# Hybrid decoder block: two of the attention's scans placed by hand in VectorE's order

## The chip, the cores and the metric

The kernel runs on one core of one Trainium2 chip, as one launch. The metric is the device time in microseconds (us). The engines are named as the profile names them: PE is TensorE, the matmul engine (PEld its weight loads), DVE is VectorE, ACT is ScalarE, POOL is GpSimd, SP is SyncE, which here issues the DMAs. All times on the trace are microseconds from the start of its span.

## What is computed

One layer of a hybrid decoder trunk over 1024 positions of width 1024: a token-mixing part (stick-breaking attention beside a Mamba-2 state-space mixer, SSD, gated and merged), cross-attention into 256 memory tokens, and a SwiGLU feed-forward, each between two RMS norms. The change touches the attention alone, 16 heads of 64 wide. For each head, query t and key s < t:

```python
z = q_t . k_s / sqrt(64)
beta = sigmoid(z)
A[t, s] = beta[t, s] * prod over s < j < t of (1 - beta[t, j])
o_t = sum over s < t of A[t, s] * v_s
```

so each row of the matrix of weights needs a running product from the diagonal leftwards over the keys.

## The kernel before

The sections follow one another: input norm and the first projections, convolution and gates (to about 655 us of the trace), the attention (657 to 1088 us, lines 750 to 954), the SSD section (from line 966), merge and output projection, cross-attention, feed-forward. Most matmuls are in fp32r and are done in three parts: an operand is split into a high part (rounded to fp32r) and a low part (what is left), and the products high x high, low x high and high x low are added up in PSUM.

**Attention.** The loop at L943 goes over 32 steps, m = 2h + half: head h, and the lower or upper 512 queries. Step m interleaves three lists of work in program order:

- `values(h, half)` (L880). For each block of 128 keys PE transposes the weights of up to four query blocks (L889) into a PSUM tile of a pool of two; ACT writes their high part `wth` (L892), DVE the low part `wtl` (L893, one input in PSUM and one in SBUF), and three blocks later PE multiplies both with the values, L901 for the high part and L902 for the low part. The lower half has four key blocks, the upper eight. Above the diagonal nothing is computed, so the last three low parts of each half have 384, 256 and 128 columns ("low384", "low256", "low128"), the others 512.
- `scores` of step m + 1 (L860). Query block b (0 to 7) has its scores against (b + 1) x 128 keys: matmuls L872 and L873, sigmoid on ACT (L874), and one scan on DVE (L875), in place on `n`, with the causal mask as second input: both inputs are in SBUF. The eight scans of a head have 128, 256, ... 1024 columns ("scan128" to "scan1024"). Those of 896 and 1024 columns belong to query blocks 6 and 7 and are issued in the step of the same head's lower half.
- one step of a dense projection (L772): q, k or gate columns of a later pair of heads. Its weight of 128 x 1024 is loaded by SP and split: the high part `whi` on ACT (L98) or on POOL (L94) in turn, the low part `wlo` on DVE (L101, two inputs in SBUF). What comes out is moved off PSUM by ACT, with a low part on DVE (L818 for q, L827 for k).

**Values.** `differences` (L845) makes the values' operand of a head on POOL: high part (L94) and low part (L101). Its tile comes from a pool of two, so it waits until PE's last product of the head before last. For every other head (a new pair) SP first loads `va` and `vb` (L851, one buffer each, free when the previous pair's low part is done), and POOL subtracts them (L852, 128 x 1024).

**Order.** What an engine executes, and in which order, is fixed when the kernel is built: a list scheduler with its own estimates of durations starts what it takes to be ready first and prefers earlier program text. So an instruction may be placed far ahead of its place in the text: the scans of 896 and 1024 columns of a head stand ahead of the last low parts of the previous head. `behind(marks)` (L204) is a context in which instructions are issued after the marked ones. When both are on one engine it sets only their order and needs no semaphore. "Head change" below means the stretch in which PE ends the values of head h - 1 and begins those of head h.

Of the kernel before, what the change touches and what calls it, by code (L numbers as in the profile page):

```python
# [8 lines left out]
F32 = mybir.dt.float32  # L9
# [3 lines left out]
ALU = mybir.AluOpType  # L13
# [3 lines left out]
P = 128  # L17
S = 1024
# [16 lines left out]
def hybrid_block(ctx, tc, a, out, dbg=None):  # L35
    nc = tc.nc
    V, A, G, T = nc.vector, nc.scalar, nc.gpsimd, nc.tensor
# [11 lines left out]
    def mk(pl, shape, dt, tag, bufs=None):  # L49
        uid[0] += 1  # L50
        kw = {} if bufs is None else {"bufs": bufs}
        return pl.tile(shape, dt, tag=tag, name=f"{tag}_{uid[0]}", **kw)
# [151 lines left out]
    def behind(marks):  # L204

        st = ExitStack()
        for m in marks:
            st.enter_context(tc.issue_after(m.ins))
        return st
# [45 lines left out]
    with ExitStack() as pa:  # L255
# [24 lines left out]
        with ExitStack() as p1:  # L280
# [135 lines left out]
            pt = mk(psp, [P, HALF], F32, "pdt", bufs=1)  # L416
# [4 lines left out]
            pt = mk(psp, [P, HALF], F32, "pv")  # L421
# [328 lines left out]
        with ExitStack() as p2:  # L750
# [13 lines left out]
            mask = mk(cb_, [P, S], BF16, "mask")  # L764
            V.memset(mask, 0.0)
            G.affine_select(mask[:, S - P:], mask[:, S - P:], [[-1, P]], ALU.is_gt, 1.0, base=0, channel_multiplier=1)

            marks, sig = [], []
            PIN = 8
            FQ = 1  # L770

# [73 lines left out]
            def differences(h):  # L845

                j = h % 2
                if j == 0:
                    va, vb = [mk(vp, [P, NCH, P], F32, n, bufs=1) for n in ("va", "vb")]
                    for t, r in ((va, 0), (vb, 1)):  # L850
                        nc.sync.dma_start(t, v_d[r:S + r, h * HD:(h + 2) * HD].rearrange("(c p) d -> p c d", p=P))  # L851
                    G.tensor_tensor(va, va, vb, ALU.subtract)  # L852
                    dvs[0] = va
                dv = dvs[0][:, :, j * HD:(j + 1) * HD]
                vt = mk(vp, [P, NCH, P], F32R, "v")
                hi_sb(vt[:, :, 0:HD], dv, "p")
                lo_of(vt[:, :, HD:P], dv, vt[:, :, 0:HD], G)
                heads[h]["v"] = vt

            def scores(h, half, tb, ns_):  # L860
                def run():
                    hd = heads[h]
                    if half == 0 and tb == 0:
                        differences(h)
                    b = half * 4 + tb
                    L = (b + 1) * P
                    nt = mk(bp, [P, (half + 1) * HALF], F32, f"n{half}")
                    ns_.append(nt)
                    for s0 in range(0, L, HALF):
                        s1 = min(L, s0 + HALF)  # L870
                        ps = mk(psc, [P, HALF], F32, "sc")[:, :s1 - s0]
                        T.matmul(ps, hd["qs"][:, b * P:(b + 1) * P], hd["kh"][:, s0:s1], start=True, stop=False)  # L872
                        marks.append(T.matmul(ps, hd["qs"][:, b * P:(b + 1) * P], hd["kl"][:, s0:s1], start=False, stop=True))  # L873
                        sig.append(A.activation(nt[:, s0:s1], ps, AF.Sigmoid, scale=-(HD ** -0.5)))  # L874
                    V.tensor_tensor_scan(nt[:, 0:L][:, ::-1], nt[:, 0:L][:, ::-1], mask[:, S - L:][:, ::-1], 1.0, ALU.mult, ALU.max)  # L875
                return run

            LAG = 3
# [1 line left out]
            def values(h, half, ns_):  # L880

                st = {}
                ni = 4 * (half + 1)

                def tr(i):
                    t0 = max(0, i - 4 * half)
                    pt = mk(pst, [P, HALF], F32, "tr")
                    for tb in range(t0, 4):
                        T.transpose(pt[:, tb * P:(tb + 1) * P], ns_[tb][:, i * P:(i + 1) * P], ident)  # L889
                    wh = mk(wt, [P, HALF], F32R, "wth")  # L890
                    wl = mk(wt, [P, HALF], F32R, "wtl")
                    A.activation(wh[:, t0 * P:], pt[:, t0 * P:], AF.Identity, bias=mone)  # L892
                    V.scalar_tensor_tensor(wl[:, t0 * P:], pt[:, t0 * P:], -1.0, wh[:, t0 * P:].bitcast(F32), ALU.add, ALU.subtract)  # L893
                    st[i] = (wh, wl, t0 * P)

                def av(i):
                    if i == 0:
                        st["po"] = mk(psv, [P, HALF], F32, "av")
                    po, vt = st["po"], heads[h]["v"]
                    wh, wl, off = st[i]  # L900
                    T.matmul(po[:, off:], vt[:, i, :], wh[:, off:], start=i == 0, stop=False)  # L901
                    marks.append(T.matmul(po[:, off:], vt[:, i, :], wl[:, off:], start=False, stop=i == ni - 1))  # L902
                    if i == ni - 1:
                        o = mk(t2, [P, HALF], F32, "oT")
                        A.activation(o, po, AF.Copy)
                        for j in range(2):
                            nc.sync.dma_start(o_d[j][h * HD:(h + 1) * HD, half * HALF:(half + 1) * HALF], o[j * HD:(j + 1) * HD])

                def step(i):
                    def run():  # L910
                        if i < ni:
                            tr(i)
                        if i >= LAG:
                            av(i - LAG)
                    return run

                return [step(i) for i in range(ni + LAG)]

            def interleave(*lists):
                items = []  # L920
                for n, (l, a0, a1) in enumerate(lists):
                    for i, f in enumerate(l):
                        items.append((a0 + (a1 - a0) * (i + 0.5) / len(l), n, f))
                for _, _, f in sorted(items, key=lambda t: t[:2]):
                    f()

            def qk_quanta(hp):

                if hp >= NH // 2:
                    return [[]] * 4  # L930
                q, k = qk_proj(hp)
                n = KT // FQ + 1
                return [q[:n], q[n:] + k[:1], k[1:n], k[n:]]
# [9 lines left out]
            for m in range(NM):  # L943
                h, half = m // 2, m % 2
                hp, r = m // 4, m % 4
                s1 = [scores((m + 1) // 2, (m + 1) % 2, tb, ns_[m + 1]) for tb in range(4)] if m + 1 < NM else []
                if r == 3:
                    nxt = qk_quanta(hp + 2)
                dn = nxt[(r + 1) % 4]
                if m >= NM - 5:  # L950
                    n = -(-len(late) // (NM - m))
                    dn, late = late[:n], late[n:]
                interleave((values(h, half, ns_[m]), 0, 1), (s1, 0, 0.7), (dn, 0, 1))
# [13 lines left out]
    with ExitStack() as p3:  # L967
# [36 lines left out]
        marks = []  # L1004
# [391 lines left out]
    marks = []  # L1396
# [506 lines left out]
```

## Time and profile before

| | us |
|---|---|
| median of 3 runs | 2554.7 |
| lowest and highest | 2552.59, 2555.76 |
| the profiled execution, device time | 2557.21 |
| its span in the trace | 2555.4 |

The profiled execution is one more run, recorded by the hardware profiler. Its span runs from the first to the last recorded instruction; durations below come from it. A row of a timeline gives start, duration, engine, line, operation, what comes out and goes in (partitions x elements), how many instructions the row joins, and in brackets how long the engine had been idle and what ended that. A row of the list of waits gives engine and tile that waited, what for, microseconds in total, times, and the longest or the mean of one. Engines work at the same time, so busy shares do not add up, and idle time of an engine that is not the bottleneck costs nothing.

### The profile page before, as it was taken

To read this page: it belongs to the slowest core of one execution; us is meant where nothing else is said; L and a number is where in the kernel's file an instruction comes from. 1 tells how busy PE (TensorE), PEld (TensorE's weight loads), DVE (VectorE), ACT (ScalarE), POOL (GpSimd) and SP (SyncE) were. 2 spreads that over 40 slices of the span, in tenths; PEclk is the share of its full clock that TensorE was granted. 3 is DMA by queue.
4 is the path that set the end of the run, shared out by engine and by line. 5 is a ranking of instruction groups with operands and counts; after the bars stand their busy time and mean duration, and the time that the engine had idled before them with its cause. 6 is when DMAs were issued, how large, how long until landed. Compare 5 with 4: busy or idle time off the path is not lost. (4 is left out here: it accounts for less than half of the span.)

```text
span 2555.4 us, 33383 instructions
## 1 busy us (share of the span) xinstructions
PE 2475.9 (97%) x12378; PEld 2033.6 (80%) x12378; DVE 1772.8 (69%) x2093; ACT 1133.7 (44%) x2023; POOL 853.9 (33%) x650
## 2 busy tenths in 40 slices
PE   7999999999999999999999999999999999999998
PEld 5788888887888878777777788887787888888876
DVE  7665777767578787688888664316459666666997
ACT  5333455555456665566554213215233333334343
POOL 3221544443121211256656040101113333323772
PEclk9999999999999999999999999999999999999999
DMA  7431443332543434365332662311232232224232
GB/s 246 152 116 55 138 149 99 99 112 90 153 112 87 120 99 104 100 207 168 107 106 65 203 209 83 124 50 34 99 116 66 83 91 75 90 91 165 99 132 99
DMA packets 255275, 293.51 MB, mean 115 GB/s; under 512 B 17023, under 2 KB 175240, under 8 KB 254986
## 3 DMA queue, kind: packets, MB, share of 16 engines
q1 hardware_dynamic: 255114, 291.40, 36.6%
q8 instruction: 97, 1.59, 0.3%
q14 instruction: 64, 0.52, 0.1%
HBM read 200.10 MB, written 74.45 MB: 107 GB/s over the span
## 5 line engine op out<-in xcount | busy, mean ns | idle before, releaser
L875 DVE TENSOR_TENSOR_SCAN n<-n,mask 128x128 f32<-128x128 f32 (+7 forms) x128 | 181.7, 1445 | 23.4 <-ACT n L874 22.2
L101 DVE TENSOR_TENSOR sw<-sf,sw 128x512 fp32r<-128x512 f32 x150 | 120.9, 818 | 82.0 <-ACT sw L98 80.5
L892 ACT ACTIVATE wth<-tr,mone 128x512 fp32r<-128x512 f32 x192 | 110.2, 584 | 81.4 <-PE tr L889 80.6
L98 ACT ACTIVATE sw<-sf 128x512 fp32r<-128x512 f32 x150 | 92.1, 626 | 113.0 <-PE mm L217 97.8
L183 POOL TENSOR_TENSOR sf<-wr,wr 128x512 f32<-128x512 f32 x38 | 59.4, 1563 | 233.4 <-DMA wr<-in_w_gu_dram 116.7
L893 DVE SCALAR_TENSOR_TENSOR wtl<-tr,wth 128x512 fp32r<-128x512 f32 x192 | 99.3, 544 | 53.9 <-ACT wth L892 53.8
L98 ACT ACTIVATE sw<-wr 128x512 fp32r<-128x512 f32 x113 | 71.2, 631 | 126.2 <-PE mm L217 125.6
L217 PE MATMUL mm<-h,sw 128*128 128x512 f32 x320 | 125.0, 392 | 1.8 <-DVE sw L101 1.8
L215 PE MATMUL mm<-h,sw 128*128 128x512 f32 x320 | 122.6, 391 | 2.9 <-ACT h L98 2.3
L216 PE MATMUL mm<-h,sw 128*128 128x512 f32 x320 | 125.3, 391 | 0.0
L101 DVE TENSOR_TENSOR sw<-wr,sw 128x512 fp32r<-128x512 f32 x113 | 106.6, 945 | 21.1 <-ACT sw L98 21.0
L669 DVE SCALAR_TENSOR_TENSOR b<-b,prmT,b 128x1023 f32<-128x1023 f32 (+2 forms) x72 | 109.6, 1522 | 15.1 <-ACT b L667 14.5
L94 POOL TENSOR_SCALAR v<-va 128x512 fp32r<-128x512 f32 x16 | 20.6, 1289 | 278.2 <-PE av L902 164.0
L874 ACT ACTIVATE n<-sc 128x512 f32<-128x512 f32 (+1 forms) x192 | 88.6, 494 | 45.5 <-PE tr L889 28.8
L152 POOL TENSOR_SCALAR rstd<-ms 128x1 f32<-128x1 f32 x74 | 28.1, 379 | 237.1 <-ACT x L1414 110.3
L104 PE MATMUL mm<-oth,bw 128*128 128x512 f32 x256 | 103.6, 405 | 3.6 <-DVE a L1214 3.6
L104 PE MATMUL p<-bw,h 128*128 128x512 f32 x256 | 98.7, 391 | 3.3 <-DVE x L1416 2.4
L105 PE MATMUL mm<-otl,bw 128*128 128x512 f32 x256 | 100.5, 393 | 0.0
L106 PE MATMUL mm<-oth,bw 128*128 128x512 f32 x256 | 100.4, 392 | 0.0
L106 PE MATMUL p<-bw,h 128*128 128x512 f32 x256 | 100.1, 392 | 0.0
L105 PE MATMUL p<-bw,h 128*128 128x512 f32 x256 | 99.9, 390 | 0.0
L185 POOL TENSOR_TENSOR sf<-wr 128x512 f32<-128x512 f32 x38 | 63.0, 1657 | 105.4 <-DVE sw L101 105.4
(616 smaller groups left out, 8044.0 us busy)
## 6 DMA issues: line engine op xcount, KB each, us to landing
wr<-in_w_gu_dram SPq DMA_DIRECT2D x80, 256.0 KB
wr<-in_w_in_dram SPq DMA_DIRECT2D x36, 512.0 KB
zr<-in_w_in_dram SPq DMA_DIRECT2D x28, 512.0 KB
gu_d<-t SPq DMA_DIRECT2D x44, 256.0 KB
wraw<-in_w_in_dram SPq DMA_DIRECT2D x20, 512.0 KB
zs_d<-zo SPq DMA_DIRECT2D x32, 256.0 KB
xs_d<-b SPq DMA_DIRECT2D x32, 256.0 KB
kl<-gt SPq DMA_DIRECT2D x64, 128.0 KB
```

The costliest lines, as they stand in the source:

```text
L98: A.activation(o, i, AF.Copy)
L101: eng.tensor_tensor(o, i, hi.bitcast(F32), ALU.subtract)
L104: first = T.matmul(ps, sh, mh, start=start, stop=False)
L105: T.matmul(ps, sh, ml, start=False, stop=False)
L106: T.matmul(ps, sl, mh, start=False, stop=stop)
L215: T.matmul(ps, w[0][:, k, :], bh, start=first and k == 0, stop=False, skip_group_check=True)
L216: T.matmul(ps, w[0][:, k, :], bl, start=False, stop=False, skip_group_check=True)
L217: ins = T.matmul(ps, w[1][:, k, :], bh, start=False, stop=last and k == 3, skip_group_check=True)
L669: V.scalar_tensor_tensor(acc[:, sh:], y[:, :S - sh], cw(3 - sh, f), acc[:, sh:], ALU.mult, ALU.add)
L875: V.tensor_tensor_scan(nt[:, 0:L][:, ::-1], nt[:, 0:L][:, ::-1], mask[:, S - L:][:, ::-1], 1.0, ALU.mult, ALU.max)
L892: A.activation(wh[:, t0 * P:], pt[:, t0 * P:], AF.Identity, bias=mone)
L893: V.scalar_tensor_tensor(wl[:, t0 * P:], pt[:, t0 * P:], -1.0, wh[:, t0 * P:].bitcast(F32), ALU.add, ALU.subtract)
```

## The change

The list `lows` collects every low-part instruction of L893. At the start of each step of the loop, `lows_done` notes the last one of the steps before and how many there are by then. In `scores`, the scan of query block 6 (896 columns) is issued behind that last low part, which in the step of a head's lower half is low128 of the previous head's upper half. The scan of query block 7 (1024 columns) is issued behind the first low part that is added after the note, the first low part (512 columns) of this head's lower half. For the first head both lists are empty. No instruction is added or taken away, and the scheduler places everything else anew around the two ties. After line 875 the changed file's lines stand one further down, after line 946 two.

```diff
-            marks, sig = [], []
+            marks, sig, lows, lows_done = [], [], [], []
...
-                    V.tensor_tensor_scan(nt[:, 0:L][:, ::-1], nt[:, 0:L][:, ::-1], mask[:, S - L:][:, ::-1], 1.0, ALU.mult, ALU.max)
+                    with behind(lows_done[:1] if b == 6 else lows[lows_done[1]:][:1] if b == 7 and lows_done else []):
+                        V.tensor_tensor_scan(nt[:, 0:L][:, ::-1], nt[:, 0:L][:, ::-1], mask[:, S - L:][:, ::-1], 1.0, ALU.mult, ALU.max)
...
-                    V.scalar_tensor_tensor(wl[:, t0 * P:], pt[:, t0 * P:], -1.0, wh[:, t0 * P:].bitcast(F32), ALU.add, ALU.subtract)
+                    lows.append(V.scalar_tensor_tensor(wl[:, t0 * P:], pt[:, t0 * P:], -1.0, wh[:, t0 * P:].bitcast(F32), ALU.add, ALU.subtract))
...
             for m in range(NM):
                 h, half = m // 2, m % 2
                 hp, r = m // 4, m % 4
+                lows_done[:] = [lows[-1], len(lows)] if lows else []
```

## The prediction

> **What bounds the kernel now.** The page comes first. TensorE (PE) is busy 97% of the span, no other engine comes near, so an edit counts only by what it does to PE's waits. The change issues the same instructions in another order, so nothing is gained in work. The second view is the list of waits over the attention section (657 to 1055 us), because it says which of PE's waits end on VectorE (DVE).
>
> ```profile
> span 2555.4 us, 33383 instructions
> PE 2475.9 (97%) x12378; PEld 2033.6 (80%) x12378; DVE 1772.8 (69%) x2093; ACT 1133.7 (44%) x2023; POOL 853.9 (33%) x650
> PE av L902 <- DVE wtl L893: 7.3, 6, 1.2
> PE tr L889 <- DVE wtl L893: 0.8, 2, 0.5
> ```
>
> Six times PE stands 1.2 us before the L902 matmul for a low part of L893, and twice 0.4 us on average in its transposes: 8.1 us is all that a better DVE order can win from PE here. The timelines show where. There are fifteen head changes, some 25 us apart, and they alternate. In six of them (702, 752, ... 952 us; call them A) POOL also splits a weight. In six more (725, 775, ... 975; call them B) ACT splits the weight, and POOL goes on to the next pair's subtraction L852. The remaining three are irregular. Here is A, on DVE, POOL, ACT and PE:
>
> ```profile
> 747.97 3.66 DVE L875 TENSOR_TENSOR_SCAN n<-n,mask 128x768 f32<-128x768 f32 x2
> 752.07 2.28 DVE L875 TENSOR_TENSOR_SCAN n<-n,mask 128x1024 f32<-128x1024 f32 x1
> 755.54 1.16 DVE L875 TENSOR_TENSOR_SCAN n<-n,mask 128x256 f32<-128x256 f32 x1
> 757.97 1.23 DVE L101 TENSOR_TENSOR wlo<-wraw,whi 128x1024 fp32r<-128x1024 f32 x1 [0.82 <-POOL whi L94]
> 759.71 0.95 DVE L875 TENSOR_TENSOR_SCAN n<-n,mask 128x384 f32<-128x384 f32 x1
> 760.58 0.59 DVE L893 SCALAR_TENSOR_TENSOR wtl<-tr,wth 128x256 fp32r<-128x256 f32 x2
> ...
> 754.05 0.71 POOL L94 TENSOR_SCALAR v<-va 128x512 fp32r<-128x512 f32 x1 [14.13 <-PE tr L889]
> 754.85 1.30 POOL L101 TENSOR_TENSOR v<-va,v 128x512 fp32r<-128x512 f32 x1
> 756.88 1.05 POOL L94 TENSOR_SCALAR whi<-wraw 128x1024 fp32r<-128x1024 f32 x1 [0.73 <-PE mm L105]
> ...
> 749.85 0.37 ACT L892 ACTIVATE wth<-tr,mone 128x128 fp32r<-128x128 f32 x1 [0.44 <-PE tr L889]
> ...
> 752.00 0.38 PE L902 MATMUL av<-wtl,v 128*128 128x256 f32 x1 [1.23 <-DVE wtl L893]
> 761.47 0.28 PE L902 MATMUL av<-wtl,v 128*128 128x256 f32 x1
> ```
>
> The first row is two scans, 768 then 896 columns, ending at 751.63; only then come the low parts, and PE waits to 752.00. And B:
>
> ```profile
> 723.75 3.68 DVE L875 TENSOR_TENSOR_SCAN n<-n,mask 128x768 f32<-128x768 f32 x2
> 727.34 0.60 DVE L893 SCALAR_TENSOR_TENSOR wtl<-tr,wth 128x256 fp32r<-128x256 f32 x2
> 728.22 2.98 DVE L875 TENSOR_TENSOR_SCAN n<-n,mask 128x1024 f32<-128x1024 f32 x2 [0.28 <-ACT n L874]
> 731.12 1.12 DVE L893 SCALAR_TENSOR_TENSOR wtl<-tr,wth 128x512 fp32r<-128x512 f32 x2
> 732.82 1.22 DVE L101 TENSOR_TENSOR wlo<-wraw,whi 128x1024 fp32r<-128x1024 f32 x1 [0.58 <-ACT whi L98]
> 733.97 0.68 DVE L818 TENSOR_TENSOR gt<-mm,qs 128x512 fp32r<-128x512 f32 x1
> 734.57 1.53 DVE L875 TENSOR_TENSOR_SCAN n<-n,mask 128x256 f32<-128x256 f32 x2
> 736.01 0.60 DVE L893 SCALAR_TENSOR_TENSOR wtl<-tr,wth 128x256 fp32r<-128x256 f32 x2
> 736.52 1.22 DVE L875 TENSOR_TENSOR_SCAN n<-n,mask 128x512 f32<-128x512 f32 x1
> 786.51 3.12 DVE L875 TENSOR_TENSOR_SCAN n<-n,mask 128x512 f32<-128x512 f32 x1
> ...
> 728.89 2.05 POOL L94 TENSOR_SCALAR v<-va 128x512 fp32r<-128x512 f32 x1 [20.65 <-PE av L902]
> 731.02 1.30 POOL L101 TENSOR_TENSOR v<-va,v 128x512 fp32r<-128x512 f32 x1
> 736.60 3.32 POOL L852 TENSOR_TENSOR va<-va,vb 128x1024 f32<-128x1024 f32 x1 [4.28 <-DMA va<-v_d]
> 786.16 2.39 POOL L852 TENSOR_TENSOR va<-va,vb 128x1024 f32<-128x1024 f32 x1 [3.83 <-DMA va<-v_d]
> ...
> 726.85 0.37 ACT L892 ACTIVATE wth<-tr,mone 128x128 fp32r<-128x128 f32 x1 [1.11 <-PE tr L889]
> ...
> 732.34 0.37 SPq L851 DMA_DIRECT2D va<-v_d  x1
> ...
> 737.27 0.28 PE L902 MATMUL av<-wtl,v 128*128 128x256 f32 x1
> ```
>
> **Scans and POOL shut each other out.** These rows decide the sign. POOL's high part takes 0.71 us in A; in B it starts 0.67 us into scan1024 (728.22, alone 2.28, so ending 730.50), takes 2.05 and ends at 730.94, 0.44 after the scan. The scan of 128 behind it ends at 731.20, 0.70 after scan1024. Scan256 of A starts while POOL's L101 runs (754.85 to 756.15) and ends at 756.70, 0.55 after it; a free pair of 256 and 384 takes 1.53, so with 0.95 less some 0.1 of overlap for 384 it is 0.68 for 256 alone. At 786.16 the subtraction came first (ends 788.55) and scan512 took 3.12 instead of 1.22, ending 1.08 later; at 736.60 the scan came first (ends 737.74) and the subtraction took 3.32 instead of 2.39, ending 2.18 later. So whoever starts first keeps the other off, and a blocked scan ends after POOL by its own time less 0.14. The Trainium skill, page "SBUF — State Buffer", section "Who interferes with whom", says that a DVE instruction with two SBUF inputs contends with a GpSimd instruction that reads SBUF, and that whoever issues first keeps the shared ports while the other fully blocks. The trace agrees on who wins; the tail of a blocked POOL part is 0.44 where the rule's whole 0.71 would stand, and with whole durations each B below would cost some 0.5 us more.
>
> **The change part by part.** It ties scan896 of head h behind the last low part of head h-1, and scan1024 behind the first low part of head h. DVE's new order at a head change is scan768, low256, low128, scan896, scan128, low512, scan1024, low384, then the weight's low part, L818 or L827, scan256, scan384, low256. What is queued behind the tied scans is therefore all of that, and PE waits for it at the second low256.
>
> *A.* Low128 follows its high part (750.22) and ends at 750.52; scan896, 2.0 us, runs 750.45 to 752.45, and PE's L902 goes at 750.6, 1.4 early. POOL's high part, freed by PE's last product, comes earlier with it, now falls into scan896 and ends at 752.45 + 0.44 = 752.9; scan128 ends at 753.15, low512 (0.6) at 753.7. POOL's L101 runs 752.95 to 754.25, as it does before 0.1 behind the high part. Scan1024 is queued at 753.7, in the middle of it, and ends at 754.25 + 2.14 = 756.4; before, it ran free. POOL's weight part, ready about 755.5 (1.4 earlier than its row), is shut out by it and ends at 757.35 (1.05 less some 0.1). Low384 fits in that gap; the weight's low part 757.35 to 758.6, L827 (0.6 net) 759.2, scan256 759.8, scan384 760.65, the first low256 to 760.95. PE takes it at 761.0 where it took it at 761.47. So of 1.4 us 0.95 is given back: **-0.45 each, six times -2.7**. Bounds: -7.3 if nothing blocks (the wait row whole); 0 if POOL's high part loses to scan128, which starts within 0.2 us of it, since the chain is then 0.4 later.
>
> *B.* The low parts wait for their high part anyway (727.22), so PE wins 0.3. Low128 ends at 727.55, scan896 runs 727.5 to 729.5, POOL's high part, freed at 728.6, ends 729.95, scan128 730.2, low512 730.75. POOL's L101 runs 730.0 to 731.3; scan1024, queued at 730.75, ends at 731.3 + 2.14 = 733.45. Low384 to 733.9, the weight's low part (before 732.82, waiting for ACT) 733.85 to 735.05, L818 735.65, scan256 queued at 735.6, 1.0 later than before. The DMA L851 is issued at the end of L101 (732.34 against 732.32), so it goes 1.0 earlier, and the subtraction is ready 3.83 to 4.28 after that end: 735.15 to 735.6 instead of 736.60. It used to fall behind scan384 (ends 736.10); now it meets scan256. If it is first, it ends at about 737.8, scan256 at 738.35, scan384 (0.85) 739.2. If scan256 is first, the subtraction ends 2.18 after it, at 738.45, and scan384 at 739.15. Either way the first low256 is there at 739.6, and PE wanted it at 737.27: **+2.3 each, six times +13.8**, from 0 (it lands after scan384 as before) to 2.8 (the subtraction at 735.6 and as long as in its longest row here, 3.32, so until 738.9, 0.5 later). The 0.8 us of the transposes' wait goes, since it came of the subtraction ahead of scan512: **-0.8**.
>
> *The last head,* at 1065 us, where DVE has slack and scan1024 fills it:
>
> ```profile
> 1065.29 2.89 DVE L875 TENSOR_TENSOR_SCAN n<-n,mask 128x1024 f32<-128x1024 f32 x1 [2.66 <-ACT n L874]
> 1070.90 2.35 DVE L1047 TENSOR_TENSOR colrows<-ident 16x1024 fp32r<-16x1024 f32 x2
> 1073.28 0.43 DVE L893 SCALAR_TENSOR_TENSOR wtl<-tr,wth 128x256 fp32r<-128x256 f32 x1
> 1073.71 1.28 DVE L1017 SCALAR_TENSOR_TENSOR wraw<-wraw,rstd,wraw 128x1024 f32<-128x1024 f32 x1
> ...
> 1075.53 0.28 PE L902 MATMUL av<-wtl,v 128*128 128x128 f32 x1
> ```
>
> Tied, scan1024 waits for a low512 that is ready only about when the scan now ends, so all of its 2.3 us comes on top: low256 ends near 1075.8 instead of 1073.71, and the order puts both L1017 (1.28 each) ahead of low128, which then ends near 1078.6. PE wanted that at 1075.53: +3.1, less some 0.5 for a wait there that the later second L1017 caused. I take **+2.5**, from 1.6 (low256 alone) to 3.1. At the irregular change near 1005 POOL's high part is long already, 1.45 us:
>
> ```profile
> 1005.11 1.45 POOL L94 TENSOR_SCALAR v<-va 128x512 fp32r<-128x512 f32 x1 [15.23 <-PE av L902]
> ```
>
> I take the middle between none and one B there, **+1.1**, and 0 at the one near 1028, where PE waits for no low part.
>
> *What else the order moves.* The 256-column scores of A go behind nine projection matmuls, one gate store on SP goes ahead of two loads, all with microseconds of slack: 0. In the SSD section a few transposes and two small products go behind other matmuls, sign unknown: 0. The stretch there has this room, so I allow 4 us to either side:
>
> ```profile
> 1090.00:1180.00 90.00, 81.31 (x627) 66.63 (x626) 78.56 (x84) 56.45 (x98) 51.57 (x41) 0.98 0.66 201
> ```
>
> The columns are the stretch, its length, busy time of PE, PE's weight loads, DVE, ACT and POOL. PE idles 8.7 us of 90.
>
> **The sum.** 13.8 - 0.8 - 2.7 + 2.5 + 1.1 = +13.9 us. The profiled run took 2557.2 for a span of 2555.4; the median of the three runs shown is 2554.7. Adding the difference to that gives 2568.6, say **2568 us**.
>
> **The rivals.**
> *The waits go and nothing follows.* The subtraction lands outside the scans and A's POOL parts do not block: -7.3 - 0.8 + 2.5 = -5.6, 2549 us. For it speaks that the subtraction misses the scans today by only 0.5 us, so small shifts decide; against it, that the two shifts (DVE 1.0 later, POOL 1.0 earlier) both push it in, and either order of arrival gives the same end. Chance 0.13.
> *Gain and loss cancel.* B is free, A gains its 2.7, the last head and 1005 cost 3.6, the transposes' 0.8 goes: 0, 2555 us. This needs the subtraction later than 736.1 on the new clock, a load 0.5 us longer than the slowest row. Chance 0.14.
> *Worse still.* As forecast, but POOL's high part loses to scan128 in A (gain 0) and the SSD section loses 4: 2568.6 + 2.7 + 4 = 2575 us. For it, the race within 0.2 us; against, no row of the SSD stretch. Chance 0.13.
> That the order does not change is ruled out: the instruction lists show it at all fifteen head changes.
>
> **How the numbers follow.** The forecast keeps 0.60. What a measurement of this kernel can tell from no change is about 0.2%, 5.1 us. Slower is forecast and worse, 0.73; same 0.14; faster 0.13. The forecast's own range is 2561 to 2573; the range of 8 in 10 takes in the worse case and reaches down towards the cancelled one: 2553 to 2577.
>
> **What would show it.** A: no wait on L902 at 752, scan1024 of some 2.7 us queued behind L101, and the second low256 within 0.5 us of its old place against PE. B: a new PE wait of about 2 us at L902 for L893, six times, near 737 plus the drift, with scan256 or scan384 stretched to over 2 us beside L852. The last head: a PE wait near 1078. If L852 starts behind scan384, B's 13.8 falls and I am wrong on the side of the rivals; if scan1024 runs free, A's gain is larger than I say.

## The result and the profile after

The changed kernel takes 2573.0 us (median of 6 runs, 2572.1 to 2578.6) against 2556.0 for the kernel before in 6 runs: a ratio of 1.0068, 95% interval 1.0057 to 1.0079, so it is slower by 17 us. The forecast was 2568 with a range of 2553 to 2577; the result lies 5 us above the forecast, at the upper end of its narrower range (2561 to 2573).

The head of its page, and from its list of waits (657 to 1110 us) the two that end on low parts (these are now L894, their products L903, the transposes L890, the scans L876):

```profile
span 2571.8 us, 33367 instructions
PE 2477.2 (96%) x12378; PEld 2033.4 (79%) x12378; DVE 1784.4 (69%) x2093; ACT 1132.1 (44%) x2023; POOL 857.6 (33%) x650
...
PE av L903 <- DVE wtl L894: 20.7, 14, 2.4
PE tr L890 <- DVE wtl L894: 0.5, 2, 0.3
```

The same 12378 matmuls are as busy as before. Over the same 657 to 1110 us the kernel before has 7.3 and 1.8 us in these two rows, so PE's waits for low parts have grown from 9.1 to 21.2 us. That the loss lies in the attention is seen from the rows of the low products, grouped by line, before and after. The times in them are the starts of the first and the last:

```profile
L902 PE MATMUL av<-wtl,v x192: 221/422/667, 682.2 to 1087.8; 128*128 128x512 f32 x96, 128*128 128x384 f32 x32, 128*128 128x256 f32 x32, 128*128 128x128 f32 x32
```

```profile
L903 PE MATMUL av<-wtl,v x192: 222/422/668, 679.7 to 1102.2; 128*128 128x512 f32 x96, 128*128 128x384 f32 x32, 128*128 128x256 f32 x32, 128*128 128x128 f32 x32
```

From the first to the last it is 405.6 us before and 422.5 after, +16.9. This stretch is used below for every run, since it leaves out what lies ahead of the attention: the first low product comes at 675.6 to 680.8 us in the ten runs below, whatever was changed in them, and at 682.2 in the trace of before. Each stretch comes from one execution, so it also holds what PE's clock did in it (last section).

**B, after** (DVE, POOL, PE at 725 us; columns as before):

```profile
724.80 2.70 DVE L876 TENSOR_TENSOR_SCAN n<-n,mask 128x896 f32<-128x896 f32 x2
728.01 2.76 DVE L876 TENSOR_TENSOR_SCAN n<-n,mask 128x1024 f32<-128x1024 f32 x1
732.87 3.53 DVE L876 TENSOR_TENSOR_SCAN n<-n,mask 128x256 f32<-128x256 f32 x2
736.32 0.59 DVE L894 SCALAR_TENSOR_TENSOR wtl<-tr,wth 128x256 fp32r<-128x256 f32 x2
...
727.32 1.30 POOL L101 TENSOR_TENSOR v<-va,v 128x512 fp32r<-128x512 f32 x1
732.62 2.38 POOL L852 TENSOR_TENSOR va<-va,vb 128x1024 f32<-128x1024 f32 x1 [4.00 <-DMA va<-v_d]
...
736.77 0.39 PE L903 MATMUL av<-wtl,v 128*128 128x256 f32 x1 [2.22 <-DVE wtl L894]
```

The subtraction starts at 732.62, a quarter of a microsecond before scan256; the pair of 256 and 384, 1.53 before, takes 3.53, and PE stands 2.22 us. Scan1024 is shut out behind L101 on the way (2.76 for 2.28).

**A, after** (750 us):

```profile
750.07 2.33 DVE L876 TENSOR_TENSOR_SCAN n<-n,mask 128x896 f32<-128x896 f32 x2
752.90 2.28 DVE L876 TENSOR_TENSOR_SCAN n<-n,mask 128x1024 f32<-128x1024 f32 x1
757.32 1.23 DVE L101 TENSOR_TENSOR wlo<-wraw,whi 128x1024 fp32r<-128x1024 f32 x1 [1.70 <-POOL whi L94]
760.51 0.60 DVE L894 SCALAR_TENSOR_TENSOR wtl<-tr,wth 128x256 fp32r<-128x256 f32 x2
...
751.98 0.83 POOL L94 TENSOR_SCALAR v<-va 128x512 fp32r<-128x512 f32 x1 [16.98 <-PE av L903]
752.90 3.37 POOL L101 TENSOR_TENSOR v<-va,v 128x512 fp32r<-128x512 f32 x1
756.24 1.05 POOL L94 TENSOR_SCALAR whi<-wraw 128x1024 fp32r<-128x1024 f32 x1
...
760.97 0.38 PE L903 MATMUL av<-wtl,v 128*128 128x256 f32 x1 [0.80 <-DVE wtl L894]
```

Scan1024 and POOL's L101 both start at 752.90. The scan has its free 2.28, and L101 takes 3.37 instead of 1.30; the weight's high part stands behind it, DVE waits 1.70 us for that, and PE 0.80 at the second low256. From the second low256 product of B to that of A it is 761.47 - 737.27 = 24.20 before and 760.97 - 736.77 = 24.20 after: A wins nothing and loses nothing. POOL's L101 takes 3.36 to 3.38 us in all six A.

### The profile page after: what moved, and what is told of

Same layout as the page of the kernel before. It is cut to its first block, busy times and chain, and to the rows that moved or that the text cites. A ratio compares the mean times of both kernels' runs of the same rounds, so it can differ in the third digit from the quotient of the medians.

```text
span 2571.8 us, 33367 instructions
## 1 busy us (share of the span) xinstructions
PE 2477.2 (96%) x12378; PEld 2033.4 (79%) x12378; DVE 1784.4 (69%) x2093; ACT 1132.1 (44%) x2023; POOL 857.6 (33%) x650
## 3 DMA queue, kind: packets, MB, share of 16 engines
q8 instruction: 97, 1.59, 0.3%
## 5 line engine op out<-in xcount | busy, mean ns | idle before, releaser
L876 DVE TENSOR_TENSOR_SCAN n<-n,mask 128x128 f32<-128x128 f32 (+7 forms) x128 | 187.4, 1486 | 11.9 <-ACT n L874 8.6
L101 DVE TENSOR_TENSOR sw<-sf,sw 128x512 fp32r<-128x512 f32 x150 | 121.8, 824 | 80.7 <-ACT sw L98 79.2
L893 ACT ACTIVATE wth<-tr,mone 128x512 fp32r<-128x512 f32 x192 | 110.3, 585 | 105.5 <-PE tr L890 104.9
L894 DVE SCALAR_TENSOR_TENSOR wtl<-tr,wth 128x512 fp32r<-128x512 f32 x192 | 101.6, 546 | 75.1 <-ACT wth L893 74.9
L101 DVE TENSOR_TENSOR sw<-wr,sw 128x512 fp32r<-128x512 f32 x113 | 107.3, 951 | 21.4 <-ACT sw L98 21.3
L94 POOL TENSOR_SCALAR v<-va 128x512 fp32r<-128x512 f32 x16 | 15.1, 948 | 290.5 <-PE av L903 290.4
L903 PE MATMUL av<-wtl,v 128*128 128x512 f32 x192 | 78.0, 407 | 20.9 <-DVE wtl L894 20.7
```

Source lines behind the costliest of these rows:

```text
L101: eng.tensor_tensor(o, i, hi.bitcast(F32), ALU.subtract)
L894: lows.append(V.scalar_tensor_tensor(wl[:, t0 * P:], pt[:, t0 * P:], -1.0, wh[:, t0 * P:].bitcast(F32), ALU.add, ALU.subtract))
```

## The experiments

Each run is compared with runs of the kernel before on its own chip; "stretch" is the one above, 405.6 before and 422.5 for the changed kernel.

**1. A short subtraction.**

```diff
-                    G.tensor_tensor(va, va, vb, ALU.subtract)
+                    G.tensor_tensor(va[:, 0:1], va[:, 0:1], vb[:, 0:1], ALU.subtract)
```

> The changed kernel with POOL's subtraction L852 done for one of its eight chunks of 128 rows instead of all (seven eighths of the subtraction are left out, the loads stay whole); the order on PE, DVE and ACT is that of the changed kernel. Theory 1 (the loss at the B head changes is the subtraction shutting out the scans of 256 and 384 columns): PE's six or seven waits of about 2.2 us at the second low256 of a B fall below 0.5 us, the pair of scans takes 1.5 us again instead of 3.5, and the time falls from 2573 to 2559 to 2562. Rival (the low part is late because scan1024 now stands ahead of it in DVE's order, whatever POOL does): the waits stay at 2.2 us, 2571 to 2575.

Measured 2557.8, ratio 1.0008 (0.9998 to 1.0019), stretch 407.9; 1.2 us below what was expected. A B in this run:

```profile
728.77 1.59 DVE L876 TENSOR_TENSOR_SCAN n<-n,mask 128x256 f32<-128x256 f32 x2
...
728.51 0.46 POOL L852 TENSOR_TENSOR va<-va,vb 128x128 f32<-128x128 f32 x1 [3.99 <-DMA va<-v_d]
...
730.73 0.38 PE L903 MATMUL av<-wtl,v 128*128 128x256 f32 x1 [0.30 <-DVE wtl L894]
```

DVE's order is that of the changed kernel, scan1024 stands as far ahead as there, and yet the pair of scans takes 1.59 and PE's wait falls from 2.22 to 0.30. The order alone is not what costs.

**2. A late load.** The load is moved, nothing is left out; PE, DVE and ACT keep the order of the changed kernel.

```diff
-                nc.sync.dma_start(dst.bitcast(F32), src.bitcast(F32))
+                mv.append(nc.sync.dma_start(dst.bitcast(F32), src.bitcast(F32)))
...
                     for t, r in ((va, 0), (vb, 1)):
-                        nc.sync.dma_start(t, v_d[...])
+                        with behind(mv[-13:][:1] if h else []):
+                            nc.sync.dma_start(t, v_d[...])
```

> The changed kernel with SP's load of va and vb tied behind the q moves that now follow it by about 2 us, all other orders as they are; nothing is left out. Theory 1 (it is when the subtraction falls that costs): the load goes 3 to 4 us later, the subtraction starts about 740 instead of 736 on the clock of before, where DVE has low parts that do not meet it; the B waits fall from 2.2 us to below 0.5 and the time to 2559 to 2563. Rival (DVE's order alone): 2571 to 2575, waits of 2.2 us. A third way: the later subtraction meets the scan of 512 or 640 columns and a new wait of 1 to 2 us appears before L890 or L902; then 2565 to 2570.

Measured 2558.8, ratio 1.0012 (1.0003 to 1.0022), stretch 408.3; just below what was expected. The load goes later than meant, and the subtraction waits for `vb` instead of `va`. The same B:

```profile
732.98 1.52 DVE L877 TENSOR_TENSOR_SCAN n<-n,mask 128x256 f32<-128x256 f32 x2
...
741.76 2.39 POOL L853 TENSOR_TENSOR va<-va,vb 128x1024 f32<-128x1024 f32 x1 [13.03 <-DMA vb<-v_d]
```

A whole subtraction, 9 us later, leaves the pair of scans alone, and PE's wait at the second low256 is 0.23 us. Two runs that take the meeting of the subtraction with the scans away in different ways, with DVE's order kept, agree, so this meeting is what B costs.

**3. Not the last head.**

```diff
-with behind(lows_done[:1] if b == 6 else ...):
+with behind([] if h == NH - 1 else lows_done[:1] if b == 6 else ...):
```

> The changed kernel without the ties for the last head only. Theory (the last head's scan1024 behind its low512 delays the low parts behind the casts and L1017 of the next section): 1.5 to 3 us less than the changed kernel, 2570 to 2571.5. Rival (PE makes it up in the next section, or the next section's own order costs the same): no difference, 2573 within 1.

Measured 2570.1, ratio 1.0057 (1.0042 to 1.0072); the medians differ by 2.9 us, though the two intervals overlap. The trace is sharper, by the second low256 products of the last two head changes:

```profile
1042.51 0.28 PE L902 MATMUL av<-wtl,v 128*128 128x256 f32 x1
1074.21 0.28 PE L902 MATMUL av<-wtl,v 128*128 128x256 f32 x1
```

```profile
1055.88 0.28 PE L903 MATMUL av<-wtl,v 128*128 128x256 f32 x1
1088.71 0.39 PE L903 MATMUL av<-wtl,v 128*128 128x256 f32 x1 [0.92 <-DVE wtl L894]
```

```profile
1056.53 0.28 PE L903 MATMUL av<-wtl,v 128*128 128x256 f32 x1
1088.30 0.28 PE L903 MATMUL av<-wtl,v 128*128 128x256 f32 x1
```

Before, changed, and without the last head's ties, the distance is 31.70, 32.83 and 31.77. It is 32.82 or 32.83 in all four traces with the last head's ties (the changed kernel, runs 1, 2 and 5) and 31.70 to 31.80 in the eight without. Behind it stands low128, which waits for the two L1019 (L1017 before), as forecast:

```profile
1088.57 2.50 DVE L1019 SCALAR_TENSOR_TENSOR wraw<-wraw,rstd,wraw 128x1024 f32<-128x1024 f32 x2
...
1091.33 0.33 PE L903 MATMUL av<-wtl,v 128*128 128x128 f32 x1 [1.02 <-DVE wtl L894]
```

From the first row of each pair above to this low128 product it is 33.02 before (to 1075.53), 35.45 after and 33.10 in this run: the last head's ties cost 2.4 us there. From low128 to the end of the span (2555.4, 2571.8, 2569.8) it is 1479.9, 1480.5 and 1480.2, and between 1477.9 and 1483.8 over all twelve traces, so nothing can be told of the next section.

The stretch of this run, 423.6, does not show the gain: its clock was halved three times instead of twice (1.5 us, last section), and one step from A to B, 760.89 to 789.52, takes 28.63 where the other five take 27.70 to 27.82; why is open.

**4. Low parts first.** Run 3's ties, and for the next head:

```diff
+lows_done[:1] if (half == 0 and b) or b == 6 else ...
```

> The changed kernel, not for the last head, with the next head's scans of 256, 384 and 512 columns tied behind the last low part of the lower half, so that low256 and low128 stand ahead of them. Theory 1: in A the second low256 no longer waits for two scans, and the 0.8 us wait there goes (A keeps its 1.4 us, about 8 us in all); in B low256 is out of the subtraction's way, but the blocked scans now stand ahead of the first low512 of the upper half, and 0.5 to 1.5 us of wait comes there; 2553 to 2560. Rival (the chain of DVE's work sets the pace, not its order): the wait moves whole to the next low part, 2569 to 2573.

Measured 2558.1, ratio 1.0008 (0.9999 to 1.0018), stretch 408.7, within the expected. PE no longer waits at L903 for L894; in B the wait moved to the transposes, as expected:

```profile
PE tr L890 <- DVE wtl L894: 8.7, 8, 1.5
```

**5. Weights on ACT.** `load_split(..., 1, "a")` in `dense`, on the changed kernel. Apart from the high parts, eight matmuls and one DVE instruction change places.

> The changed kernel with every weight of the attention's dense projections split on ACT (the high part L94 of POOL in A becomes L98 on ACT). Theory 2 (A gives its 1.4 us back because scan1024 and POOL's L101 are ready at the same moment, the scan wins, and the weight's high part queued behind L101 comes 2 us late): DVE no longer waits 1.7 us for the weight, the 0.8 us wait of PE at the second low256 of A goes, 0.8 to 1.4 us of each of six A stays won, 2564 to 2569. Rival (DVE's work between the two low256 is simply too much for A, or ACT's extra 1 us delays a high part): the wait stays or moves, 2571 to 2574.

Measured 2566.3, ratio 1.0038 (1.0025 to 1.0052), stretch 416.2: 6.3 us won. The same A:

```profile
756.40 1.50 DVE L101 TENSOR_TENSOR wlo<-wraw,whi 128x1024 fp32r<-128x1024 f32 x1 [0.23 <-ACT whi L98]
...
753.44 3.38 POOL L101 TENSOR_TENSOR v<-va,v 128x512 fp32r<-128x512 f32 x1
...
760.32 0.39 PE L903 MATMUL av<-wtl,v 128*128 128x256 f32 x1
```

L101 on POOL is still shut out for 2 us, but no weight stands behind it; DVE waits 0.23 instead of 1.70, and PE's row shows no wait. Theory 2 held: A's gain went into POOL's queue. From the second low256 of a B to that of the next A it is now 23.00 or 23.01 three times, 1.2 less than before. The other two, 24.53 and 24.52, stand behind a halved clock (last section). In B, PE's wait is still 2.2 to 2.4 us.

**6 and 7. Edits joined.** Run 4 with the late load, and that with the weights on ACT.

> Low parts first and not for the last head, as in the run before, with SP's load of va and vb tied behind the q moves as well. By theory 1 the 8.7 us of waits in PE's transposes for L894, which the subtraction leaves in B, go almost whole: 2550 to 2553, 4 to 6 us below the kernel before. Rival (the waits come of the three scans standing ahead of low512, not of the subtraction): 2557 to 2559.

> The same with the weights split on ACT as well: if both theories hold, A keeps its whole 1.4 us: 2544 to 2549. If only theory 1 holds, as the run before it, 2550 to 2553.

The first gave 2556.5, ratio 0.9993 (0.9984 to 1.0002), stretch 405.7, 3.5 us above what was expected and near the rival's 2557. The second gave 2552.1, ratio 0.9978 (0.9968 to 0.9987), stretch 399.7: in the range named for theory 1 alone, not in the 2544 to 2549 of both. The wait of the transposes is still there, 6.7 and 5.9 us. It has changed its cause, as a B of run 7 shows:

```profile
740.78 2.88 DVE L877 TENSOR_TENSOR_SCAN n<-n,mask 128x640 f32<-128x640 f32 x1
...
739.90 2.41 POOL L853 TENSOR_TENSOR va<-va,vb 128x1024 f32<-128x1024 f32 x1 [12.85 <-DMA vb<-v_d]
...
744.29 0.44 PE L891 MATMUL tr<-ident,n 128*128 128x128 f32 x2 [1.11 <-DVE wtl L895]
```

The late subtraction meets the scan of 640 columns (1.49 in the changed kernel) instead of those of 256 and 384; in run 6 this scan takes 3.30 at the same B. It is the third way named for run 2.

**8. The late load in the kernel before.**

> The kernel before with SP's load tied as in the late load, nothing else. Theory 1: the subtraction misses the scans of 256 and 384 columns there already, so only the 0.8 us of the transposes' wait can go: 2554.5 to 2556.5, no change that can be told. Rival (the late load gains by itself, whatever the order of the scans): 2545 or below.

Measured 2553.5, ratio 0.9984 (0.9975 to 0.9993), stretch 406.2. It neither gains in the attention nor reaches the rival's 2545; the 0.16% below the kernel before do not come from the stretch, and what they are is left open. So a difference of this size in the total alone says little about an edit.

**9 and 10. The load in between, and the scans spread.** Run 7 with only `va`'s load tied, behind `mv[-14]`, and that with scan384 and scan512 of the next head tied behind the first and second low512 of the upper half.

> The run with all three edits, with only the load of va tied, and behind the first of the two q moves: the load goes some 1 us earlier and does not share the queues with vb. In the run with all three, the subtraction ran from 739.90 to 742.31 and kept the scan of 640 columns (740.78, 2.88 us instead of 1.49) and the low part behind it, a wait of 1.1 us in PE's transposes in each B. Theory 1: the subtraction now falls at 736 to 739, between the scan of 512 and that of 640, beside low parts alone; the 5.9 us of waits of L891 for L895 go to below 2, and the time is 3.5 to 5.5 us below that run: 2546.5 to 2548.5 where it was 2552.05. Rival (the transposes wait for something else than the shut-out scan of 640): the wait stays, no difference to that run.

> As the load in between, and the next head's scans of 384 and 512 columns tied behind the first and second low512 of the upper half, so that they stand among the low parts. Theory 1: in B they now meet the subtraction at 736 to 739, one of them is shut out by 1 to 2 us, and the low512 behind it is late; 1 to 4 us above the load in between. Rival (spreading the scans among the low parts helps, as DVE has gaps there): up to 2 us below it.

They gave 2553.3 (0.9993, 0.9984 to 1.0002; stretch 405.4) and 2552.7 (0.9983, 0.9974 to 0.9992; stretch 402.7). In run 9 the transposes' wait fell from 5.9 to 2.8 us, and 1.9 of what is left is a single wait at 691 us, so in B it had been the shut-out scan. But waits for the moves of the next heads' k took its place:

```profile
PE tr L891 <- DVE wtl L895: 2.8, 3, 1.9
PE sc L874 <- DMA kl<-gt: 2.7, 6, 0.6
```

The wait at 691 us is the same meeting once more, at the first head change:

```profile
685.56 4.80 DVE L877 TENSOR_TENSOR_SCAN n<-n,mask 128x256 f32<-128x256 f32 x3
...
685.80 2.63 POOL L853 TENSOR_TENSOR va<-va,vb 128x1024 f32<-128x1024 f32 x1 [35.26 <-DMA va<-v_d]
...
691.00 0.88 PE L891 MATMUL tr<-ident,n 128*128 128x128 f32 x4 [1.88 <-DVE wtl L895]
```

The three scans take 2.65 in run 7, where the subtraction starts 2.1 us after the first of them (684.03, 686.12) instead of 0.24. With the halved clock behind it (last section) run 9 loses 3.7 us against run 7 from its first low product to the second low256 of the first A, and the expected 3.5 to 5.5 us did not come. Run 10 came out 0.6 us below run 9, on its rival's side, within the intervals.

Run 7 has the shortest stretch and the lowest ratio of the runs that keep the whole computation, but its interval overlaps those of runs 8 and 10.

## Why the prediction was right, point by point

**B, +13.8: right, in mechanism and size.** The moments of the second low256 product, before and after, give the cost of each B; two of them:

```profile
761.47 0.28 PE L902 MATMUL av<-wtl,v 128*128 128x256 f32 x1
787.27 0.28 PE L902 MATMUL av<-wtl,v 128*128 128x256 f32 x1
811.89 0.28 PE L902 MATMUL av<-wtl,v 128*128 128x256 f32 x1
```

```profile
788.65 0.39 PE L903 MATMUL av<-wtl,v 128*128 128x256 f32 x1 [2.28 <-DVE wtl L894]
814.40 0.38 PE L903 MATMUL av<-wtl,v 128*128 128x256 f32 x1 [0.80 <-DVE wtl L894]
```

From A at 760.97 to the B at 788.65 it is 27.68 after and 25.80 before, +1.88. The six come to +12.9. The mechanism is the forecast one: the load goes early, scan256 goes late, and the subtraction meets the scans. At some B it starts first, at others scan256 does (942.11 against 942.16, 995.57 against 995.84); the pair of scans takes 3.53 to 3.74 us either way, as forecast. Runs 1 and 2 took the meeting away in two ways and the wait went with it.

**The transposes, -0.8: right.** Their wait stood in the stretches from B to the next A, 24.62 and 24.81 us before at 787 and 937 us, where the other three are 24.15 to 24.20. Against the 24.20 of the changed kernel at full clock that is 1.0 less, and in run 1, which has the full clock there, the two are 24.19 and 24.16.

**A, -2.7: wrong in the mechanism, and 0 in size.** The step that failed is that POOL's high part would fall into scan896 and hold scan128. It started at 751.98, only 0.1 us before scan896 (2.02 us alone) ended, and scan128 went ahead of it: the two scans took 2.33, as they do at 1015.15 with POOL idle, and the high part ended 0.41 after them, at 752.81. So L101 was ready 0.45 us later than forecast and scan1024 0.3 us earlier (this trace runs 0.50 us ahead of the one before at this point), both at 752.90. Scan1024 was to meet L101 in its middle and be shut out; it met it at its start and went first. The forecast's own figures pointed there: 754.05 less 1.4 is 752.65, behind the 752.45 at which its scan896 ends. The end is the bound given for a high part that loses to scan128, 0, though not by the path I had described there: not the scan came late, but the weight behind L101. A reading was off as well, though the sum does not use it: the 0.71 us of POOL's high part is not its free time, since it begins at 754.05, before scan1024 ends (752.07 + 2.28). Where no scan shuts it out, as at 1017.53 in the changed kernel, it takes 0.63.

**The last head, +2.5: right.** By run 3 it is 2.4 at low128, where the forecast had it, and by the way it named. The SSD section, forecast 0, and all that follows come to +0.6 in this trace, less than the traces differ there.

**The change near 1005, +1.1: right in size by luck, wrong in the mechanism.** With the second low256 products of B at 987.23 and of this change at 1012.74 before, 999.59 and 1026.08 after, the distance grows from 25.51 to 26.49, +0.98. The forecast was a middle between none and one B, but no subtraction runs here. What happens is what happens in A, the weight's high part behind a shut-out L101:

```profile
1018.24 3.14 POOL L101 TENSOR_TENSOR v<-va,v 128x512 fp32r<-128x512 f32 x1
1021.36 1.04 POOL L94 TENSOR_SCALAR whi<-wraw 128x1024 fp32r<-128x1024 f32 x1
...
1022.44 1.23 DVE L101 TENSOR_TENSOR wlo<-wraw,whi 128x1024 fp32r<-128x1024 f32 x1 [1.70 <-POOL whi L94]
```

In run 5, with the weight on ACT, the same distance is 25.53.

**Not foreseen: +3.0** from PE's clock after the waits, below. The sum then is 12.9 - 1.0 + 0 + 2.4 + 0.6 + 1.0 + 3.0 = 18.9, less 2.5 for the earlier start of this span: 16.4, and the spans differ by 16.4. Against the 13.9 of the forecast 5.0 more were lost: 2.7 that A did not win, 3.0 of the clock and 0.6 behind the last head, less 1.3 by which the other terms came out lower. The medians differ by 17.1.

**The rivals.** "Nothing follows" fell, since the subtraction did meet the scans in every B. Run 2 is "gain and loss cancel" made on purpose, with the load later than the forecast had it, and comes out at 1.0012. "Worse still", 2575, is 2 us from the result, nearer than the forecast. The half of it that concerns A came true; the 4 us in the SSD section did not show, and the clock stood in their place, which no rival named.

## What to carry to other kernels

A tie that moves work within one engine's order also moves what that work shuts out: before tying, list what other engines run at the new place, their queues and the DMAs that start them, and not only the wait that goes. Here a low part that PE needs stood behind scans that are needed later. Putting the low part first, keeping the weight off the queue that is shut out, and moving the transfer that starts the subtraction shortened the stretch by 5.9 us and gave 0.22% below the kernel before (0.13 to 0.32); the ties alone, 0.68% above it. In these runs much of the time freed at one place was spent at the next collision, so measure a fixed stretch of the trace beside the total, and compare single steps in it, since one execution's clock is in the stretch too.

## What the runs showed of the hardware

PE's clock can be halved for a while behind a wait of about 2 us. In the changed kernel the B at 788 us is followed by this (windows of 1 us; start and end, length, busy time of PE, PEld, DVE, ACT, POOL, then the granted clock, the DMA share and GB/s):

```profile
789.00:790.00 1.00, 1.00 (x9) 0.92 (x8) 0.93 (x1) 0.41 (x1) 0.00 (x0) 0.98 0.98 269
790.00:791.00 1.00, 1.00 (x4) 0.73 (x3) 0.69 (x1) 0.28 (x1) 0.00 (x0) 0.50 0.41 122
791.00:792.00 1.00, 1.00 (x6) 0.89 (x5) 0.00 (x1) 0.21 (x1) 0.00 (x0) 0.50 0.00 0
792.00:793.00 1.00, 1.00 (x6) 1.00 (x5) 0.00 (x0) 0.74 (x2) 0.00 (x0) 0.50 0.00 0
793.00:794.00 1.00, 1.00 (x6) 0.89 (x5) 0.64 (x1) 0.83 (x2) 0.00 (x0) 0.81 0.42 98
```

The clock is 0.50 for some 3.4 us, from 790 to past 793. Such a slow phase costs 1.5 us: in the changed kernel the step from a B to the next A is 25.75 and 25.69 us behind the two slow phases (788.65 to 814.40, and the one to 971.83) and 24.19 to 24.20 the other three times. In run 3 it is 25.73 to 25.76 behind three and 24.19 to 24.20 twice, in run 5 24.52 to 24.53 behind two and 23.00 to 23.01 three times. It happened after two of the six waits of the changed kernel, which were all of 2.2 to 2.4 us, so the length of the wait does not decide it alone. In run 9 it followed the wait of 1.88 at 691 us: the clock is 0.50 from there to past 694. In runs 1, 2, 4, 6, 7, 8 and 10, whose waits there are at most 1.7 us, the granted clock was 1.00 over 690 to 1000 us. At the end of the attention, where PE waits 1.9 to 2.5 us for ACT, it is 0.50 in all twelve traces, from the wait on or at most 2.3 us behind it. That the wait is the cause rests on this coming together; no run tried it by itself. The Trainium skill, page "TensorE: Matmul & The Clock Gate", section "Part 1: The HAM clock gate", says that the clock halves after an idle window of about 3.4 us, and that the window runs free of the work. The 3.4 us of slow clock and its turning up after only some of the waits agree; waits of 2.28 and 1.88 us that were followed by it are shorter than the page's window.
